# Four more k tiles of a down projection by seven products: a first group of half size in an encoder block's feed-forward part

## The chip, the core and the metric

The kernel runs on one core of a Trainium2 chip. The metric is the device time of one launch in microseconds (us), median of several runs. Engines are named as in the profile: PE is TensorE (the matrix unit), PEld its weight load, DVE is VectorE, ACT is ScalarE, POOL is GpSimd, SP is SyncE, which here only issues transfers.

## What is computed

One layer of an encoder over 256 tokens of width 2048, in float32. Attention with a window and a Fourier mixing part come first; the part that matters here is the feed-forward block behind them (5504 = 43 x 128 hidden features):

```python
h = _rmsnorm(x, norm2_g)
up = h @ w_up                                  # 2048 x 11008
gate, val = up[..., :D_FF], up[..., D_FF:]
gate = depthwise_conv(gate, dw_w, width 3) + dw_b
act = gelu(gate) * val                         # 256 x 5504
x = x + act @ w_down                           # 5504 x 2048: the down projection
y = _rmsnorm(x, normf_g)
```

## The kernel before

**Two parts of every operand.** A float32 matrix is split into a high part (rounded to a shorter format) and a low part (the rest). A product is three matmuls: high x high, low x high, high x low. The high part of a weight tile is made by ACT (a copy, L168, or L944 for the products' weights), the low part by DVE (a subtraction, L169 or L945). High and low tiles have three buffers each, shared by all kinds of units, so the split for item n + 2 can start when item n - 1 has left PE.

**Items.** From the feed-forward part on, the work is a list of items made by `ff_items`. One item is one stretch of matmuls on PE:

- *gate j* or *val j*: the up projection of one 128-feature tile, 32 matmuls (`still_weights`, L321), on 1 MB of weights.
- *product*: one of the seven products of a Strassen-like scheme for a group of the down projection. The activations of a group of 8 feature tiles are seen as a 2 x 2 block matrix (two halves of 4 tiles by two halves of 128 tokens), the weights likewise (two halves of 4 tiles by two column blocks of 512, `c` and `c + 2`). Seven products in place of eight, for each c in 0, 1. A product runs over 4 tiles, 3 matmuls each: 12 matmuls (`by_parts`, L1053 to L1055).
- *down*: a late unit. Feature tiles 32 to 39 go the plain way, in two sets of 4: per set, four units (one for each block of 512 columns), each 4 tiles x 2 token halves x 3 = 24 matmuls (`moving_weights`, L304 to L306).
- *last*: feature tiles 40 to 42, plain too, at the very end (`last_product`, L1192 to L1194), followed by the final norm.

Four groups cover tiles 0 to 31. While the 14 products of a group run, the up units of the next 8 tiles stand between them: `PATTERN` is `"uuu" + "su" * 13 + "s"` (u an up unit, s a product). After the last group's products come four late units, the six up units of tiles 40 to 42, four late units, four last units.

**What goes on beside PE.** `ff_step(n)` first issues what evicts the results of item n - 1 (`beside`), then the split of item n + 2, then what can wait (`behind`). The order is written out by hand; each engine works through its instructions in that order. Per up unit, DVE and ACT combine the two halves of the result (L833 to L836), run the convolution and GELU (L843 to L854) and multiply (L874; for the late and last tiles L866, with a split of the activations at L878 and L879). Per group, `operand` (L901, L902) and `operand_sums` make the seven left operands over seven steps. The products P1 and N5 stay in four banks of PSUM over all groups; the others are added to the residual `xs` or to the tiles Z when they end (`product_out`, L1022 to L1028). After the last product of a column block `shared_out` adds what is shared (L1036 to L1047, eight additions of 128x512 in three steps). `down_out` (L1060) adds a late unit to `xs`.

**The ring of product weights.** Per group and c, four weight tiles a, b, d, c are loaded by SP into two buffers (`ring_load`, L928), each when the split of an earlier one has freed its buffer. Sums of weights are made in part by POOL's accumulating transfers, which read a tile from HBM and add it in place: into b after `first_sums` (L959 and the transfer behind it), into the sum x after the split for N5 (L949) and after that for P6 (L951).

**Transfers of the other weights.** `split(i)` issues the load of unit i + 3 on SP (L152).

**The end.** `last_post` adds a last unit to `xs` (L1068), sums squares on ACT (L1072), and multiplies by the gain on POOL (L1080; the gain `gfb` is loaded by POOL at L1170, at the first late unit). The squares of the last column block are summed by DVE (L1085), those of blocks 1 and 2 are added by `other_squares` (DVE, L1090), and POOL takes the power (L1097); then the rows are scaled (L1106 to L1110) and stored.

**The q and k units** of the attention part also use `still_weights`. `QK_FIRST` says how many high and low parts each of them runs before it alternates.

Of the kernel before, what the change touches and what calls it, by code (L numbers as in the profile page):

```python
# [61 lines left out]

N_GROUPS = 4
LATE = [list(range(32, 36)), list(range(36, 40))]
LAST = list(range(40, NF))
# [3 lines left out]

PATTERN = "uuu" + "su" * 13 + "s"  # L70


def ff_items():


    def ups(tiles):
        return [(kind, j) for j in tiles for kind in ("gate", "val")]

    items = ups(range(8))
    for g in range(N_GROUPS):  # L80
# [4 lines left out]
        items += [todo[c].pop(0) for c in PATTERN]  # L85
        assert not any(todo.values())
    items += [("down", 0, c) for c in range(4)] + ups(LAST)
    items += [("down", 1, c) for c in range(4)] + [("last", c) for c in range(4)]
    return items


@with_exitstack
def block_kernel(
# [7 lines left out]
    w_out: bass.AP,  # L101
    w_up: bass.AP,
    w_down: bass.AP,
    w_down_late: bass.AP,
# [27 lines left out]
    for n, it in enumerate(items):  # L132
        if it[0] == "product":
            continue
        up_index[n] = len(units)
        if it[0] in ("gate", "val"):
            units.append((w_up[2 * it[1] + (it[0] == "val")], 2048))
            shifts.append((0, SHIFT))
            continue
        elif it[0] == "down":  # L140
            units.append((w_down_late[4 * it[1] + it[2]], 2048))
        else:
            units.append((w_down_last[it[1]], 512 * len(LAST)))
        shifts.append((0, 0))
# [589 lines left out]
    for n, (kind, h) in enumerate(QK_ORDER):  # L734

        def work(hi, lo):
            ps = st["ps", kind, h] = bank(mm, f"ps_{kind}{h}")
            still_weights(hi, lo, ps, range(NK), QK_FIRST.get(n, (0, 0)))

        unit(N_QK + n, work)  # L740
# [116 lines left out]
    def val_mult(j):  # L857
        va, ge = sums_of.pop(f"v{j}"), gate_out.pop(j)
        g, q = divmod(j, 8)
        if j >= 8 * N_GROUPS:  # L860
            if q % 2 == 0 or j == LAST[0]:
                tag = ("va", "va", "op_P1", "op_N3", "op_P7", "op_N5")[(j - 32) // 2]
# [7 lines left out]
        if q % 4 == 0:  # L870
            parts[g, q // 4] = fp.tile(
                [P, 4, S], F32, tag="va", name=f"va{g}k{q // 4}", bufs=3
            )
        nc.vector.tensor_tensor(parts[g, q // 4][:, q % 4, :], va, ge, ALU.mult)  # L874

# [17 lines left out]
    def block_of(g, name):  # L893
        k, t = PLACE[name]
        return parts[g, k][:, :, t * P : (t + 1) * P]

    def operand(g, name):

        o = fp.tile([P, 2, 4, P], F32R, tag=f"op_{name}", name=f"op_{name}", bufs=1)
        a = block_of(g, name)  # L900
        nc.scalar.activation(o[:, 0], a, AF.Copy)  # L901
        nc.vector.tensor_tensor(o[:, 1], a, f32(o[:, 0]), ALU.subtract)  # L902
        parts[name] = o
# [12 lines left out]

    ring, ring_tiles = [(g, c, w) for g in range(N_GROUPS) for c in range(2) for w in "abdc"], {}
    ring_next = [0]

    def weights_of(g, c, w):  # L920
        return w_down[(g * 2 + c) * 4 + "abcd".index(w)]

    def ring_load():
        if ring_next[0] < len(ring):
            key = ring[ring_next[0]]
            ring_next[0] += 1
            ring_tiles[key] = fp.tile([P, 2048], F32, tag="rawd", name="rawd%d%d%s" % key)
            nc.sync.dma_start(ring_tiles[key], weights_of(*key))  # L928
# [3 lines left out]
    def split_product(g, c, p):  # L932

        raw = {w: ring_tiles.get((g, c, w)) for w in "abcd"}
        x = ring_tiles["x"]
        src = {"P1": raw["a"], "N3": raw["d"], "P7": raw["b"], "P2": raw["c"]}.get(p, x)
        hi, lo = (
            wp.tile([P, 2176], F32R, tag=h, name=f"{h}_{p}_{g}{c}", bufs=3)[
                :, PRODUCT_SHIFT : PRODUCT_SHIFT + 2048
            ]  # L940
            for h in ("hi", "lo")
        )
        halves["product", g, c, p] = (hi, lo)
        nc.scalar.activation(hi, src, AF.Copy)  # L944
        nc.vector.tensor_tensor(lo, src, f32(hi), ALU.subtract)  # L945
        if p in ("P1", "P7", "N3", "P2"):
            ring_load()
        elif p == "N5":
            nc.gpsimd.dma_start(x, weights_of(g, c, "d"), accum_op=ALU.add)  # L949
        elif p == "P6":  # L950
            nc.gpsimd.dma_start(x, weights_of(g, c, "c"), accum_op=ALU.add)  # L951
        elif p == "N4" and (g, c) != (N_GROUPS - 1, 1):
            pending.append(lambda: first_sums(g + c, 1 - c))

    def first_sums(g, c):

        a, b = ring_tiles[g, c, "a"], ring_tiles[g, c, "b"]
        x = ring_tiles["x"] = fp.tile([P, 2048], F32, tag="sumw", name=f"sumw{g}{c}", bufs=1)
        nc.vector.tensor_tensor(x, a, b, ALU.add)  # L959
# [26 lines left out]
    def up_posts(n, kind, j, ps):  # L986
# [4 lines left out]
        else:  # L991
            at(beside, n + 1, scaled_sum, ps, f"v{j}")
            at(beside, n + 2, val_mult, j)
            if j % 8 == 7 and j < 8 * N_GROUPS:
                g = j // 8
                at(behind, n + 1, operand, g, "P1")
# [7 lines left out]
                at(behind, n + 7, operand, g, "P6")  # L1004
            if j >= 8 * N_GROUPS:
                at(behind, n + 2, act_parts, j)
# [41 lines left out]

    def by_parts(ps, o, hi, lo, first, last):

        for p in range(4):
            s = slice(p * 512, (p + 1) * 512)
            nc.tensor.matmul(ps, o[:, 0, p, :], hi[:, s], start=first and p == 0, stop=False)  # L1053
            nc.tensor.matmul(ps, o[:, 1, p, :], hi[:, s], start=False, stop=False)  # L1054
            nc.tensor.matmul(ps, o[:, 0, p, :], lo[:, s], start=False, stop=last and p == 3)  # L1055

# [8 lines left out]
    def last_post(c, b, ps, o=0, n=512):  # L1065
# [47 lines left out]

    pair = []
    for q in range(2):
# [17 lines left out]
    for n, it in enumerate(items):  # L1133
        if n < 2:
            continue
        if it[0] == "last":
            break
        if n in (8, 9):
            ring_load()
        if n == 13:  # L1140
            pending.append(lambda: first_sums(0, 0))
# [7 lines left out]
        if it[0] == "product":  # L1149
            kind, g, c, p = it  # L1150
            end = g == N_GROUPS - 1
            if (c, p) in held:
                by_parts(held[c, p], parts[p], *halves.pop(it), g == 0, end)
            else:
                ps = bank(mm, f"ps_{p}{g}{c}")
                by_parts(ps, parts[p], *halves.pop(it), True, True)
                at(beside, n + 1, product_out, g, c, p, ps)
            if end and p == "N4":
                for q in range(3):
                    at(behind, n + 1 + q, shared_out, c, q)  # L1160
        else:
            kind, g, c = it
# [58 lines left out]
def _layout(inp):  # L1221
# [40 lines left out]
    def rows_by(tiles, cols):  # L1262
# [4 lines left out]
    downs = [  # L1267
        rows_by(range(k, k + 4), c + n)
        for g in range(N_GROUPS)
        for c in (0, 512)  # L1270
        for k in (8 * g, 8 * g + 4)
        for n in (0, 1024)
    ]
    late = [rows_by(fs, 512 * c) for fs in LATE for c in range(4)]
    dw = f(inp["dw_w"]).reshape(3, NF, P).transpose(2, 1, 0).reshape(P, 3 * NF)
# [23 lines left out]
        "w_up": wup,  # L1299
        "w_down": np.stack(downs),  # L1300
        "w_down_late": np.stack(late),
# [22 lines left out]
```

## Time and profile before

| what | value |
|---|---|
| median of 3 runs (lowest, highest) | 947.45 us (947.23, 947.6) |
| the profiled execution | 947.17 us |
| its span, first to last instruction | 945.4 us |
| mean granted TensorE clock | 0.998 |
| PE, DVE, ACT, POOL busy | 935.7, 749.1, 534.2, 45.1 us |
| read from HBM | 208.79 MB, 223 GB/s over the span |

How to read it: a row of the list of groups names line, engine, operation, output and input, shape, count, then the busy time in us and the mean of one in ns, then the idle time of the engine ahead of it. A row of the chain gives start, length and what ran. A row of a timeline gives the same for one engine; what stands in brackets is the idle time ahead and what ended it. Rows of the list of waits give the total in us, how often, and the longest.

### The profile page before, as it was taken

How to read it: one execution, taken by the hardware profiler on the slowest of the kernel's cores; microseconds unless marked ns; L12 is line 12 of the kernel's file. 1: busy time of each engine (PE TensorE's matmuls, PEld its weight loads, DVE VectorE, ACT ScalarE, POOL GpSimd, SP SyncE). 2: the span in 40 equal slices, each digit the busy share in tenths (PEclk: the TensorE clock that was granted, in tenths of full speed). 3: DMA queues.
4: the chain of work that ended last, by engine and by line, in shares of the span. 5: the costliest groups of instructions: out<-in, count | busy, mean ns of one | idle time of the engine just before them, and what ended most of it. 6: DMA issues, size and time to landing. Idle time of an engine off the chain costs nothing.

```text
span 945.4 us, 12773 instructions
## 1 busy us (share of the span) xinstructions
PE 935.7 (99%) x5081; PEld 811.6 (86%) x5081; DVE 749.1 (79%) x932; ACT 534.2 (56%) x646; POOL 45.1 (5%) x59
## 2 busy tenths in 40 slices
PE   9999999999999999999999999999999999999996
PEld 7889998888888888888888888888888888888885
DVE  7668877566676689787898978988879979888776
ACT  7756766454454546556565555665556755553442
POOL 0100000000000000000000000000000000000002
PEclk9999999999999999999999999999999999999999
DMA  9964444446556675978778797877977697776532
GB/s 366 306 223 148 164 152 160 147 169 219 179 178 230 255 227 189 290 241 264 227 260 246 238 306 232 267 231 233 296 251 249 205 298 219 223 246 216 181 134 89
DMA packets 32189, 211.72 MB, mean 224 GB/s; under 512 B 3553, under 2 KB 4065, under 8 KB 8065
## 3 DMA queue, kind: packets, MB, share of 16 engines
q1 hardware_dynamic: 28448, 184.55, 53.2%
q0 software_dynamic: 3680, 26.35, 14.8%
q8 instruction: 40, 0.66, 0.3%
q14 instruction: 21, 0.16, 0.0%
HBM read 208.79 MB, written 2.10 MB: 223 GB/s over the span
## 4 chain that ended last, share of the span: by engine, by line
PE 98%; issue 1%; DMA 0%; DVE 0%; POOL 0%; ACT 0%; DVEq 0%; POOLq 0%; ACTq 0%
PE ps_gate L321 25%; PE ps_val L321 25%; PE ps_q L321 7%; PE ps_P L1055 3%; PE ps_P L1054 3%; PE ps_P L1053 3%; PE ps_a L306 2%; PE ps_a L304 2%; PE ps_k L321 2%; PE ps_N L1055 2%; PE ps_a L305 2%; PE ps_N L1054 2%; PE ps_N L1053 2%; PE ps_l L304 2%; PE ps_l L305 2%; PE ps_l L306 2%
## 5 line engine op out<-in xcount | busy, mean ns | idle before, releaser
L169 DVE TENSOR_TENSOR lo<-raw,hi 128x2048 fp32r<-128x2048 f32 (+1 forms) x133 | 302.7, 2276 | 53.8 <-ACT hi L168 53.7
L168 ACT ACTIVATE hi<-raw 128x2048 fp32r<-128x2048 f32 (+1 forms) x133 | 253.2, 1904 | 57.5 <-PE ps_l L305 22.8
L321 PE MATMUL ps_gate<-hU,hi 128*128 128x512 f32 x688 | 236.2, 389 | 0.0
L321 PE MATMUL ps_val<-hU,hi 128*128 128x512 f32 x688 | 236.2, 389 | 0.0
L321 PE MATMUL ps_gate<-hU,lo 128*128 128x256 f32 x688 | 189.9, 276 | 0.0
L321 PE MATMUL ps_val<-hU,lo 128*128 128x256 f32 x688 | 189.9, 276 | 0.0
L321 PEld LDWEIGHTS ps_gate<-hU,hi 128*128 128x128 f32 x688 | 129.2, 188 | 26.8
L321 PEld LDWEIGHTS ps_val<-hU,hi 128*128 128x128 f32 x688 | 129.1, 188 | 26.8
L321 PEld LDWEIGHTS ps_gate<-hU,lo 128*128 128x128 f32 x688 | 129.1, 188 | 1.1
L321 PEld LDWEIGHTS ps_val<-hU,lo 128*128 128x128 f32 x688 | 129.2, 188 | 1.1
L833 ACT ACTIVATE ft_g<-ps_gate 128x256 f32<-128x256 f32 x43 | 16.5, 384 | 120.0 <-PE ps_gate L321 119.8
L833 ACT ACTIVATE ft_v<-ps_val 128x256 f32<-128x256 f32 x43 | 16.5, 384 | 88.0 <-PE ps_val L321 88.0
L321 PE MATMUL ps_q<-hT,hi 128*128 128x512 f32 x192 | 66.2, 393 | 0.0
L321 PE MATMUL ps_q<-hT,lo 128*128 128x256 f32 x192 | 52.3, 277 | 0.0
L1053 PE MATMUL ps_P<-hi_P,op_P 128*128 128x512 f32 x128 | 49.8, 389 | 0.0
L1054 PE MATMUL ps_P<-hi_P,op_P 128*128 128x512 f32 x128 | 49.8, 389 | 0.0
L1055 PE MATMUL ps_P<-lo_P,op_P 128*128 128x512 f32 x128 | 49.8, 389 | 0.0
L945 DVE TENSOR_TENSOR lo_N<-sumw,hi_N 128x2048 fp32r<-128x2048 f32 x16 | 36.6, 2290 | 10.1 <-ACT hi_N L944 10.1
L321 PEld LDWEIGHTS ps_q<-hT,hi 128*128 128x128 f32 x192 | 35.7, 188 | 6.9
L304 PE MATMUL ps_a<-hi,cat 128*128 128x512 f32 x96 | 37.9, 395 | 0.0
L306 PE MATMUL ps_a<-lo,cat 128*128 128x512 f32 x96 | 37.5, 390 | 0.0
L835 DVE TENSOR_TENSOR fa_g<-ps_gate,ft_g 128x256 f32<-128x256 f32 x43 | 18.2, 422 | 24.3 <-ACT ft_g L833 24.3
(333 smaller groups left out, 1603.6 us busy)
## 6 DMA issues: line engine op xcount, KB each, us to landing
raw<-in_w_up SPq DMA_DIRECT2D x86, 1024.0 KB, 5.1
raw<-in_w_in SPq DMA_DIRECT2D x20, 1024.0 KB, 4.9
raw<-in_w_out SPq DMA_DIRECT2D x16, 1024.0 KB, 4.8
sumw<-in_w_down POOLq DMA_DIRECT2D x16, 1024.0 KB, 8.6
raw<-in_w_down_late SPq DMA_DIRECT2D x8, 1024.0 KB, 4.8
raw<-in_w_down_last SPq DMA_DIRECT2D x4, 768.0 KB, 4.2
ux<-in_w_u_x SPq DMA_DIRECT2D x3, 768.0 KB, 9.2
xs<-in_x SPq DMA_DIRECT2D x4, 512.0 KB, 16.5
```

The source lines that it names most:

```text
L168: nc.scalar.activation(hi[:, 0:n], raw[:, 0:n], AF.Copy)
L169: nc.vector.tensor_tensor(lo[:, 0:n], raw[:, 0:n], f32(hi[:, 0:n]), ALU.subtract)
L304: nc.tensor.matmul(ps, ah, wh, start=first and q == q0, stop=False)
L305: nc.tensor.matmul(ps, al, wh, start=False, stop=False)
L306: nc.tensor.matmul(ps, ah, wl, start=False, stop=last and q == q0 + len(kk) - 1)
L321: nc.tensor.matmul(ps[:, x], (hi, lo)[i][:, k * P : (k + 1) * P], hk(k)[:, x], start=n == 0 and k == 0, stop=n == len(order) - 1 and k == ...
L833: nc.scalar.activation(tmp, ps[:, S : 2 * S], AF.Copy)
L835: nc.vector.tensor_tensor(add, ps[:, 0:S], tmp, ALU.add)
L945: nc.vector.tensor_tensor(lo, src, f32(hi), ALU.subtract)
L1053: nc.tensor.matmul(ps, o[:, 0, p, :], hi[:, s], start=first and p == 0, stop=False)
L1054: nc.tensor.matmul(ps, o[:, 1, p, :], hi[:, s], start=False, stop=False)
L1055: nc.tensor.matmul(ps, o[:, 0, p, :], lo[:, s], start=False, stop=last and p == 3)
```

## The change

The down projection gets five groups in place of four: a first one of half size (two halves of 2 tiles, tiles 0 to 3) and four of full size (tiles 4 to 35). Only tiles 36 to 39 remain for late units, four of them, and these no longer follow the products: in the last group's pattern they stand among the last products, as do the six up units of tiles 40 to 42. A product of the half group is 6 matmuls on half a weight tile (128x1024). In the last group, the products P2 and N4 of column block c are not evicted: the late unit for c (0 or 1) adds to their two banks, and one `down_out` evicts both. The closing sums of c = 1 are issued after P6 already, one step in every two items. The first loads of the ring come at items 2 and 3, the first sum at item 5. `gfb` is loaded at the late unit for c = 1. At the end, the squares of blocks 1 and 2 of the second token half are added by POOL, each as it comes, in place of one DVE operation. All q and k units but two now run one high part ahead.

```diff
-QK_FIRST = {0: (1, 0), 2: (1, 0), 4: (1, 0), 5: (1, 0), 6: (1, 0), 8: (2, 2), 10: (2, 2), 12: (2, 2), 14: (1, 0)}
+QK_FIRST = {n: (2, 2) if n in (8, 12) else (1, 0) for n in range(16)}
...
-N_GROUPS = 4
-LATE = [list(range(32, 36)), list(range(36, 40))]
+GROUPS = [(0, 2), (4, 4), (12, 4), (20, 4), (28, 4)]
+LATE = list(range(36, 40))
...
-PATTERN = "uuu" + "su" * 13 + "s"
+PATTERNS = ["uuu" + "su" * 13 + "s"] * (len(GROUPS) - 1)
+PATTERNS += ["uuu" + "su" * 6 + "sd" + "su" * 5 + "sdsdd"]
...
+    firsts = [first for first, _ in GROUPS] + [LATE[0], NF]
+    items = ups(0, firsts[1])
+    for g, pattern in enumerate(PATTERNS):
         todo = {
-            "u": ups(range(8 * g + 8, 8 * g + 16)),
+            "u": ups(firsts[g + 1], firsts[g + 2]),
             "s": [("product", g, c, p) for c in range(2) for p in PRODUCTS[c]],
+            "d": [("down", c) for c in (0, 2, 1, 3)],
         }
...
-    items += [("down", 0, c) for c in range(4)] + ups(LAST)
-    items += [("down", 1, c) for c in range(4)] + [("last", c) for c in range(4)]
+    return items + [("last", c) for c in range(4)]
...
     def operand(g, name):
         o = fp.tile([P, 2, 4, P], F32R, tag=f"op_{name}", name=f"op_{name}", bufs=1)
+        o = o[:, :, 0 : GROUPS[g][1], :]
...
+    def ring_tile(g, tag, name, bufs):
+        t = fp.tile([P, 2048], F32, tag=tag, name=name, bufs=bufs)
+        return t[:, 0 : 512 * GROUPS[g][1]]
...
-    def by_parts(ps, o, hi, lo, first, last):
-        for p in range(4):
+    def by_parts(ps, o, hi, lo, n, first, last):
+        for p in range(n):
...
+        if (c, b) == (1, 1):
+            nc.gpsimd.tensor_tensor(
+                ssq3[:, b, 3:4], ssq3[:, b, 3:4], ssq3[:, b, 1:2], ALU.add
+            )
...
-        if n in (8, 9):
+        if n in (2, 3):
             ring_load()
-        if n == 13:
+        if n == 5:
             pending.append(lambda: first_sums(0, 0))
...
+            elif end and p in ("P2", "N4"):
+                ps = joined[c, p] = bank(mm, f"ps_{p}{g}{c}")
+                by_parts(ps, parts[p], *halves.pop(it), GROUPS[g][1], True, False)
...
-            if end and p == "N4":
+            if end and p == ("N4", "P6")[c]:
                 for q in range(3):
-                    at(behind, n + 1 + q, shared_out, c, q)
+                    at(behind, n + 1 + (1 + c) * q, shared_out, c, q)
...
-            ps = [bank(mm, f"ps_l{g}{c}{b}") for b in range(2)]
+            if c < 2:
+                ps = [joined.pop((c, p)) for p in ("P2", "N4")]
+            else:
+                ps = [bank(mm, f"ps_l{c}{b}") for b in range(2)]
             for b in range(2):
-                moving_weights(hi, lo, 512, LATE[g], act.get, b, ps[b], True, True)
+                moving_weights(hi, lo, 512, LATE, act.get, b, ps[b], c >= 2, True)
             at(beside, n + 1, down_out, c, ps)
-            if (g, c) == (0, 0):
+            if c == 1:
                 gfb = fp.tile([P, D], F32, tag="sumw", name="gfb", bufs=1)
                 nc.gpsimd.dma_start(gfb, normf_g.partition_broadcast(P))
...
-    v = other_squares(1, add_squares(1, 0, 256, ssq3[:, 1, 3:4], 4))
+    v = add_squares(1, 0, 256, ssq3[:, 1, 3:4], 4)
+    nc.gpsimd.tensor_tensor(v, v, ssq3[:, 1, 2:3], ALU.add)
```

The rest of the diff lays the weights out to match (a `w_down_two` of eight half tiles, `w_down` of 32 tiles, `w_down_late` of four) and passes the group's size along.

More of the change, by code (lines that the diff above doesn't have):

```diff
@@ L68, with group_of, ups @@
 ]
-PATTERN = "uuu" + "su" * 13 + "s"
-def ff_items():
[L76 to L80, printed above, removed]
+PATTERNS = ["uuu" + "su" * 13 + "s"] * (len(GROUPS) - 1)
+PATTERNS += ["uuu" + "su" * 6 + "sd" + "su" * 5 + "sdsdd"]
+def group_of(j):
+    for g, (first, n) in enumerate(GROUPS):
+        if j < first + 2 * n:
+            return (g, *divmod(j - first, n))
+    return None
+def ff_items():
+    def ups(first, end):
+        return [(kind, j) for j in range(first, end) for kind in ("gate", "val")]
+    firsts = [first for first, _ in GROUPS] + [LATE[0], NF]
+    items = ups(0, firsts[1])
+    for g, pattern in enumerate(PATTERNS):
         todo = {
-            "u": ups(range(8 * g + 8, 8 * g + 16)),
+            "u": ups(firsts[g + 1], firsts[g + 2]),
             "s": [("product", g, c, p) for c in range(2) for p in PRODUCTS[c]],
+            "d": [("down", c) for c in (0, 2, 1, 3)],
         }
-        items += [todo[c].pop(0) for c in PATTERN]
-        assert not any(todo.values())
-    items += [("down", 0, c) for c in range(4)] + ups(LAST)
-    items += [("down", 1, c) for c in range(4)] + [("last", c) for c in range(4)]
-    return items
+        items += [todo[c].pop(0) for c in pattern]
+        assert not (todo["u"] or todo["s"]), (g, todo)
+    return items + [("last", c) for c in range(4)]
 @with_exitstack
@@ L140, in block_kernel @@
         elif it[0] == "down":
-            units.append((w_down_late[4 * it[1] + it[2]], 2048))
+            units.append((w_down_late[it[1]], 2048))
         else:
@@ L737, in work @@
             ps = st["ps", kind, h] = bank(mm, f"ps_{kind}{h}")
-            still_weights(hi, lo, ps, range(NK), QK_FIRST.get(n, (0, 0)))
+            still_weights(hi, lo, ps, range(NK), QK_FIRST[n])
         unit(N_QK + n, work)
@@ L869, in val_mult @@
             return
[L870 to L874, printed above, removed]
+        g, half, q = group_of(j)
+        if q == 0:
+            parts[g, half] = fp.tile([P, 4, S], F32, tag="va", name=f"va{g}k{half}", bufs=3)
+        nc.vector.tensor_tensor(parts[g, half][:, q, :], va, ge, ALU.mult)
     def act_parts(j):
@@ L913, in operand_sums @@
             tt(a01, a00, a01, ALU.add)
-    ring, ring_tiles = [(g, c, w) for g in range(N_GROUPS) for c in range(2) for w in "abdc"], {}
+    ring, ring_tiles = [(g, c, w) for g in range(len(GROUPS)) for c in range(2) for w in "abdc"], {}
     ring_next = [0]
     def weights_of(g, c, w):
-        return w_down[(g * 2 + c) * 4 + "abcd".index(w)]
+        n = c * 4 + "abcd".index(w)
+        return w_down_two[n] if g == 0 else w_down[8 * (g - 1) + n]
+    def ring_tile(g, tag, name, bufs):
+        t = fp.tile([P, 2048], F32, tag=tag, name=name, bufs=bufs)
+        return t[:, 0 : 512 * GROUPS[g][1]]
     def ring_load():
@@ L951, in split_product @@
             nc.gpsimd.dma_start(x, weights_of(g, c, "c"), accum_op=ALU.add)
-        elif p == "N4" and (g, c) != (N_GROUPS - 1, 1):
+        elif p == "N4" and (g, c) != (len(GROUPS) - 1, 1):
             pending.append(lambda: first_sums(g + c, 1 - c))
@@ L957, in first_sums @@
         a, b = ring_tiles[g, c, "a"], ring_tiles[g, c, "b"]
-        x = ring_tiles["x"] = fp.tile([P, 2048], F32, tag="sumw", name=f"sumw{g}{c}", bufs=1)
+        x = ring_tiles["x"] = ring_tile(g, "sumw", f"sumw{g}{c}", 1)
         nc.vector.tensor_tensor(x, a, b, ALU.add)
@@ L993, in up_posts @@
             at(beside, n + 2, val_mult, j)
-            if j % 8 == 7 and j < 8 * N_GROUPS:
-                g = j // 8
+            if j + 1 in [first + 2 * n for first, n in GROUPS]:
+                g = group_of(j)[0]
                 at(behind, n + 1, operand, g, "P1")
@@ L1054, in by_parts @@
             nc.tensor.matmul(ps, o[:, 1, p, :], hi[:, s], start=False, stop=False)
-            nc.tensor.matmul(ps, o[:, 0, p, :], lo[:, s], start=False, stop=last and p == 3)
+            nc.tensor.matmul(ps, o[:, 0, p, :], lo[:, s], start=False, stop=last and p == n - 1)
     def down_out(c, pss):
@@ L1111, in scaled @@
         nc.sync.dma_start(out[b * P : (b + 1) * P, k : k + n], y)
-    pair = []
+    pair, joined = [], {}
     for q in range(2):
@@ L1267, in _layout @@
     downs = [
-        rows_by(range(k, k + 4), c + n)
-        for g in range(N_GROUPS)
+        rows_by(range(k, k + m), c + n)
+        for first, m in GROUPS
         for c in (0, 512)
-        for k in (8 * g, 8 * g + 4)
+        for k in (first, first + m)
         for n in (0, 1024)
     ]
-    late = [rows_by(fs, 512 * c) for fs in LATE for c in range(4)]
+    late = [rows_by(LATE, 512 * c) for c in range(4)]
     dw = f(inp["dw_w"]).reshape(3, NF, P).transpose(2, 1, 0).reshape(P, 3 * NF)
```

28 lines of the change are left out of this document (15 added, 13 removed).

## The prediction, made before the changed kernel ran

> **What bounds the kernel now.** I read the page first: busy shares, then the chain that ended last. Then the list of what TensorE (PE) waited for, because a busy share of 99% can hide short stalls.
>
> ```profile
> PE 935.7 (99%) x5081; PEld 811.6 (86%) x5081; DVE 749.1 (79%) x932; ACT 534.2 (56%) x646; POOL 45.1 (5%) x59
> PE 98%; issue 1%; DMA 0%; DVE 0%; POOL 0%; ACT 0%; DVEq 0%; POOLq 0%; ACTq 0%
> ```
>
> ```profile
> PE ps_warm L249 <- POOL ones L241: 1.0, 1, 1.0
> PE ps_u L383 <- ACT hT L256: 0.6, 1, 0.6
> ```
>
> The second fence is the whole list of PE's waits: 1.6 us, both at the very start. From the first weights on PE never waits for an engine or a transfer. So the time is the number of matmuls times their pitch, plus a short start and a tail after the last matmul. A change gains only by taking matmuls away or shortening the tail, and it loses only if something that is now hidden comes late.
>
> **The pitch.** Successive matmuls overlap in the trace, so the printed duration of one is not its cost. The cost is the distance between starts, which the chain in order of time gives.
>
> ```profile
> 828.36 5.44 PE ps_gate L321 x32
> 836.52 5.44 PE ps_val L321 x32
> 866.47 5.46 PE ps_gate L321 x32
> ```
>
> A gate or value unit (32 matmuls) takes 5.44 us, and the next begins 8.16 us after it. The 2.72 us between are one product: 4 k tiles of 3 matmuls, 12 in all, so 0.2267 us for each 512-wide matmul. The four late units follow the last product, from 836.52 + 5.44 + 2.72 = 844.68 to 866.47: 21.79 us for 96 matmuls, 0.227 each. The two ways of doing the down projection pay the same per matmul, and opening one more product has no price of its own (at most 0.01 us).
>
> **The change: matmuls.** Four k tiles cost 4 units x 24 = 96 matmuls by the plain way. As a half group they cost 14 products x 2 tiles x 3 = 84. Twelve matmuls go: 12 x 0.2267 = **-2.72 us**. Nothing else on PE changes in number.
>
> **Order of the q and k units.** In sixteen units only the order of the same matmuls changes. PE waits for nothing there, so there is no wait to remove.
>
> ```profile
> 59.49 5.47 PE ps_q L321 x32
> 65.41 5.49 PE ps_q L321 x32
> ```
>
> The first of these has the plain alternation, the second one high part ahead: 0.02 us apart. Eight units change, so between -0.2 and +0.2 us; I take 0.
>
> **What hides the vector work.** Every weight needs a high part on ACT and a low part on DVE before PE may use it. The half group adds 14 half-size splits and drops four full ones.
>
> ```profile
> L169 DVE TENSOR_TENSOR lo<-raw,hi 128x2048 fp32r<-128x2048 f32 x130 | 297.5, 2288 | 52.3 <-ACT hi L168 52.1
> L377 DVE TENSOR_TENSOR lo<-ux,hi 128x1024 fp32r<-128x1024 f32 x4 | 4.9, 1222 | 0.7 <-ACT hi L376 0.7
> L835 DVE TENSOR_TENSOR fa_v<-ps_val,ft_v 128x256 f32<-128x256 f32 x43 | 18.2, 423 | 14.3 <-ACT ft_v L833 14.3
> L1028 DVE TENSOR_TENSOR xs<-ps_N,xs 128x512 f32<-128x512 f32 x16 | 10.9, 684 | 0.0
> ```
>
> ```profile
> 360.00:469.00 109.00, 109.00 (x588) 94.29 (x587) 90.38 (x90) 66.11 (x65) 4.26 (x5) 1.00 0.77 244
> 735.00:845.00 110.00, 110.00 (x593) 95.13 (x592) 97.81 (x109) 66.27 (x66) 4.85 (x6) 1.00 0.76 235
> ```
>
> In the windows view the columns are sum, PE, weight loads, DVE, ACT, POOL, clock, DMA share, GB/s. The first window is the first group, the second the last group. In the **half group** PE's time for the same steps falls to 14 x 1.36 + 13 x 5.44 = 89.8 us. DVE's 90.38 loses 14 x (2.29 - 1.22) = 15.0 on splits, 1.1 on the sum of two weights, and 11 x (0.68 - 0.42) = 2.9 on operands: 71.4 us, 80% of PE's time against 83% now. In the **last group** two up units go out of the stretch (4.0 us of DVE each: a split of 2.29, four 0.42-us operations), four late units come in (2.29 + 2 x 0.68 each, 14.6), four products lose their eviction because they share a bank with a late unit (-2.7), and the closing sums of the second column now fall inside (8 x 0.68 = 5.5): 97.8 - 8.0 + 14.6 - 2.7 + 5.5 = 107.2 us. PE's time there is 14 x 2.72 + 15 x 5.44 = 119.7, so 90% against 89% now. DVE does not become the bound in either stretch.
>
> An average can still hide one late split. How early are they? In a quiet pair:
>
> ```profile
> 379.56 5.44 PE ps_val L321 x32
> 382.23 2.29 DVE L169 TENSOR_TENSOR lo<-raw,hi 128x2048 fp32r<-128x2048 f32 x1
> 387.72 5.44 PE ps_gate L321 x32
> ```
>
> The low part for the unit at 387.72 was ready at 384.52, 5.0 us after the unit before it began. In the half group the next unit begins after 6.80 us instead of 8.16, so some 1.8 us are left. The tightest place that I found is in the last group:
>
> ```profile
> 743.53 2.28 DVE L169 TENSOR_TENSOR lo<-raw,hi 128x2048 fp32r<-128x2048 f32 x1
> 745.73 0.69 DVE L902 TENSOR_TENSOR op_N<-va3k,op_N 128x512 fp32r<-128x512 f32 x1
> 746.83 0.28 PE L321 MATMUL ps_gate<-hU,lo 128*128 128x256 f32 x1
> ```
>
> There 1.0 us is left (ready 745.81, used 746.83). The changed kernel has the same steps at this place, since the first three up units and the first six pairs of the last group keep their order. In the half group's own operand steps the DVE work shrinks with the window. So I cost the vector work at nothing; if the cover fails by a microsecond or two at one place, that is the price, once. No bank is waited for either: the late unit for column block 3 takes the two banks of block 2, freed a whole product and a unit earlier.
>
> **Transfers that move.** The first weights of the half group are loaded six items earlier, on SP's queue ahead of loads for up units; the final gain is loaded later, on POOL's queue, behind the last accumulating transfers.
>
> ```profile
> raw<-in_w_up SPq DMA_DIRECT2D x86, 1024.0 KB, 5.1
> gfb<-in_normf_g POOLq DMA_DIRECT2D x1, 1024.0 KB, 4.6
> ```
>
> Up weights are loaded three units ahead (3 x 5.44 = 16.3 us) and land in 5.1, so two half loads in front, each at most another 5.1, use up only part of the 11 us that are left. The gain can be issued when the last product's weight is split. From there PE still has that product, two late units and the first last product, 2.72 + 2 x 5.44 + 2.04 (9 matmuls) = 15.6 us, before POOL multiplies by it: 4.6 us of landing fit. Both cost nothing.
>
> **The tail.** On POOL two 128x1 additions are new, and one DVE operation (L1090) goes.
>
> ```profile
> 935.81 0.19 ACT L1072 ACTIVATION_READ_ACCUMULATOR junkc<-xs 128x1 f32 x1
> 937.04 0.19 ACT L1072 ACTIVATION_READ_ACCUMULATOR junkc<-xs 128x1 f32 x1
> ```
>
> ```profile
> 936.76 0.48 DVE L1085 CUSTOM_DVE_ANT_0 z_P<-xs,ssq 128x256 f32<-128x256 f32 x1
> 937.17 0.08 DVE L1085 DVE_READ_ACCUMULATOR2_ANT ssq<- 128x1 f32 x1
> 937.37 0.27 DVE L1090 TENSOR_SCALAR ssq<-ssq 128x1 f32<-128x1 f32 x1
> 937.56 0.41 DVE L1068 TENSOR_TENSOR xs<-ps_e,xs 128x256 f32<-128x256 f32 x1
> 938.00 0.48 DVE L1085 CUSTOM_DVE_ANT_0 z_P<-xs,ssq 128x256 f32<-128x256 f32 x1
> ```
>
> ```profile
> 931.06 0.57 POOL L1097 TENSOR_TENSOR rstd<-ssq,half_pow 128x1 f32<-128x1 f32 x1 [1.11 <-DVE ssq L1090]
> 938.58 0.55 POOL L1097 TENSOR_TENSOR rstd<-ssq,half_pow 128x1 f32<-128x1 f32 x1 [4.55 <-DVE ssq L1085]
> ```
>
> ```profile
> 937.06 0.28 PE L1194 MATMUL ps_e<-lo,act 128*128 128x256 f32 x1
> ```
>
> A 128x1 operation on POOL took 0.55 us here; the additions are not in this trace, so I price them like it. The first can start at 936.0 (ACT's result) and ends about 936.6, ahead of its use at 936.76. The second can start at about 937.3 and ends about 937.9, when DVE wants it at 938.0; meanwhile DVE, free of L1090, does its addition up to 0.15 us earlier. Queued behind each on POOL is only the other and the power. Both ends: -0.15 us, or +0.55 if one addition lies wholly on the path. I take 0.
>
> The sum: 947.17 (the profiled execution: span 945.4 and 1.8 around it) - 2.72 = 944.45. The median of the runs is 947.45, 0.28 above the profiled one, which gives 944.73. I forecast **944.6 us**.
>
> **A rule that speaks against it.** The tail's rows show when POOL and DVE get in each other's way:
>
> ```profile
> 931.15 0.69 DVE L1068 TENSOR_TENSOR xs<-ps_e,xs 128x512 f32<-128x512 f32 x1 [0.17 <-PE ps_e L1194]
> 932.74 1.29 POOL L1080 TENSOR_TENSOR xs<-xs,gfb 128x512 f32<-128x512 f32 x1 [1.11 <-ACT junkc L1072]
> 932.77 1.81 DVE L1106 SCALAR_TENSOR_TENSOR xs<-xs,rstd,gfb 128x512 f32<-128x512 f32 x1
> 939.43 2.07 DVE L1106 SCALAR_TENSOR_TENSOR xs<-xs,rstd,gfb 128x512 f32<-128x512 f32 x3
> ```
>
> Three such DVE operations alone took 2.07 us, one beside POOL's took 1.81: about 1.1 us lost. As a mechanism of this kernel: if a new POOL addition starts just ahead of a DVE operation on SBUF, DVE stands for its 0.55 us; both on the path give 944.6 + 1.1 = 945.7, one gives 945.15. Against it: during the second addition DVE adds from PSUM, and such an addition at 931.15, beside POOL's power at 931.06, took its ordinary 0.69. The Trainium skill, page "SBUF — State Buffer", section "Who interferes with whom", says that POOL and a DVE operation with two SBUF inputs take one shared port as an exclusive lock, and the later one waits to the end. By that rule the new additions could hold the squares at 936.76; the trace agrees in the 1.81 us.
>
> **The rivals.**
> (a) *Late splits.* The last group, at 90%, with 1.0 us of slack, or the half group, with 1.8, makes PE wait a few times. For: the closing sums now run among splits. Against: all the sums above. Price 0.5 to 2.5 us: 945.1 to 947.1.
> (b) *The POOL lock*, as priced: 945.15 to 945.7.
> (c) *The half group does not halve.* If a product had a fixed cost of 0.19 us, 14 more of them would eat the 2.72: 947.2. Against: the 0.01 us above.
> (d) *Slower: accumulating transfers land late in the half group.*
>
> ```profile
> sumw<-in_w_down POOLq DMA_DIRECT2D x16, 1024.0 KB, 8.6
> rawd10b<-in_w_down POOLq DMA_DIRECT2D x1, 1024.0 KB, 10.5
> ```
>
> POOL adds a weight tile from HBM into the sum between N5's split and P6's, and again between P6's and N4's. In three of four cases these now lie 2 x 6.80 = 13.6 us apart, not 16.3. N5's split takes some 2.7 of them, and a late split still has some 4 us before PE wants it, so PE waits once a landing takes over about 14.9 us. Each microsecond above costs up to 3. From 16.4 us of landing on, the result is over 0.2% slower (3 x 1.55 = 4.6 us); at 17 it is 951. Against: 8.6 is the median and 10.5 the worst for twice the bytes.
>
> **How the numbers follow.** About 0.2% (1.9 us) is what a measurement can tell from no change. My forecast, 944.2 to 945.1, has 0.72: PE's arithmetic is exact and only hidden work can spoil it. (b) 0.05, (a) 0.13, (c) 0.04, (d) 0.06. Faster by over 0.2%, below 945.55: 0.72, 0.05 and 0.05 of (a), 0.82. Same: the rest of (a) and (c), 0.12. Slower: 0.06. The range goes from 944.0 (both gains of order and tail) to 946.4 (most of (a)), which leaves out 0.06, 0.04 and some 0.05 of (a).
>
> **What would show it.** Right: PE's list of waits still has only the two rows of the start; products of the first group last 1.36 us in the chain, so their pairs recur every 6.80; the last matmul ends 2.7 us earlier; the tail after it is as long as now (945.4 - 937.34 = 8.1 us). Wrong: a PE wait for a low part (L181 or L962 of the changed kernel) proves (a); a DVE split of the first group that waits for a transfer, with PE waiting behind it, proves (d); a longer stretch between the last matmul and the last power on POOL proves (b).

## The result, and the profile after

The changed kernel takes **945.76 us** (median of 18 runs, 945.2 to 947.13) against 947.4 for the kernel before (18 runs, 946.81 to 948.04): a ratio of 0.9982, 95% interval 0.9975 to 0.9988. It is faster by 1.6 us. The forecast was 944.6 with a range of 944.0 to 946.4, so the sign is as forecast, the time lies in the range, and 1.2 us of the expected gain are missing.

The page of the kernel after: its busy time by engine, and the chain that ended last by engine.

```profile
PE 934.7 (99%) x5069; PEld 809.9 (86%) x5069; DVE 759.8 (81%) x948; ACT 541.4 (57%) x659; POOL 50.6 (5%) x67
...
PE 98%; DVE 1%; DMA 0%; issue 0%; ACT 0%; DVEq 0%; POOLq 0%; POOL 0%; ACTq 0%
```

Its PE has twelve matmuls fewer, 5069 for 5081, as the change says. At 0.2267 us each they should take 2.72 us with them, but PE's busy time fell by 1.0 only. The list of what PE waited for does not tell where the rest is:

```profile
PE ps_warm L261 <- POOL ones L253: 1.0, 1, 1.0
PE ps_u L395 <- ACT hT L268: 0.2, 1, 0.2
```

It is whole, and again has only the two rows of the start. So PE waits for nothing and yet is longer busy than its matmuls account for: the matmuls themselves must have become longer. The chain in order of time shows where. First the half group (start, length, what ran):

```profile
317.12 0.23 PE ps_P L1070
...
318.48 5.44 PE ps_val L333 x32
...
325.28 5.44 PE ps_gate L333 x32
...
332.08 5.44 PE ps_val L333 x32
```

A pair recurs every 6.80 us, so a product of the half group takes 1.36, exactly half. Then the last group:

```profile
842.08 5.44 PE ps_gate L333 x32
...
850.24 0.23 PE ps_P L316
850.47 0.24 PE ps_P L317
...
855.71 0.23 PE ps_P L1070
...
858.47 5.60 PE ps_val L333 x32
...
866.85 5.60 PE ps_gate L333 x32
...
875.22 5.60 PE ps_val L333 x32
...
883.59 5.60 PE ps_gate L333 x32
...
891.97 5.60 PE ps_val L333 x32
```

L316 and L317 are the first late unit, L1070 the product behind it. From there on a unit of the same 32 matmuls takes 5.60 us, not 5.44, and a pair recurs every 8.37, not 8.16. I call this the **slow stretch**. It runs from 855.8 to 902.3, into the second token half of the late unit for block 2; the product and the first half of the late unit behind that are slow again (905.9 to 910.5); then all is normal. Lengths there above the usual ones: five up units at 0.16, the products between them at 0.055, the edges; together 1.3 us. I call a start **slow** when it comes later behind the one before than the usual 226.7 ns for 512 columns or 113.3 ns for 256, and count what it is late by. Behind 266 us of the span, and without one break of 0.1 us near 267 that both kernels have, slow starts add up to 0.18 us in before and to 1.44 in after.

What else differs between the normal stretch ahead of it and the slow one of equal length? The windows view (sum, PE, weight loads, DVE, ACT, POOL, clock, DMA share, GB/s), the normal stretch first:

```profile
801.20:847.60 46.40, 46.40 (x255) 40.34 (x254) 41.26 (x43) 27.56 (x30) 1.72 (x2) 1.00 0.75 234
855.80:902.20 46.40, 46.40 (x241) 39.48 (x240) 40.69 (x45) 26.61 (x23) 1.72 (x2) 1.00 0.69 222
```

Then two groups by form (busy time, mean ns of one, idle time), in the normal stretch and, in the fence behind it, in the slow one:

```profile
L333 PE MATMUL ps_val<-hU,hi 128*128 128x512 f32 x48 | 16.5, 389 | 0.0
...
L333 PEld LDWEIGHTS ps_val<-hU,lo 128*128 128x128 f32 x48 | 9.0, 188 | 0.1
```

```profile
L333 PE MATMUL ps_val<-hU,hi 128*128 128x512 f32 x48 | 16.9, 395 | 0.0
...
L333 PEld LDWEIGHTS ps_val<-hU,lo 128*128 128x128 f32 x48 | 9.0, 188 | 0.1
```

The granted clock is 1.00 in both, the transfers and DVE do less in the slow one, the weight loads are equal at 188 ns. Only the matmuls are longer, 395 ns for 389, with nothing in these views that would explain it.

The span fell by 1.7 us, from 945.4 to 943.7: -2.72 for the matmuls, +1.26 for slow starts, +0.17 because the v units began that much later (27.10 for 26.93; in the runs below it lies between 26.82 and 27.56 whatever the change), -0.05 on the q and k units, -0.31 behind the start of the last matmul. That is -1.65.

### The profile page after: what moved, and what is told of

Same layout as the page of the kernel before. It is cut to its first block, busy times and chain, and to the rows that moved or that the text cites. A ratio compares the mean times of both kernels' runs of the same rounds, so it can differ in the third digit from the quotient of the medians.

```text
span 943.7 us, 12802 instructions
## 1 busy us (share of the span) xinstructions
PE 934.7 (99%) x5069; PEld 809.9 (86%) x5069; DVE 759.8 (81%) x948; ACT 541.4 (57%) x659; POOL 50.6 (5%) x67
## 4 chain that ended last, share of the span: by engine, by line
PE 98%; DVE 1%; DMA 0%; issue 0%; ACT 0%; DVEq 0%; POOLq 0%; POOL 0%; ACTq 0%
PE ps_val L333 25%; PE ps_gate L333 25%; PE ps_q L333 7%; PE ps_P L1071 3%; PE ps_P L1072 3%; PE ps_P L1070 3%; PE ps_N L1071 3%; PE ps_N L1072 3%; PE ps_N L1070 3%; PE ps_a L318 2%; PE ps_a L316 2%; PE ps_k L333 2%; PE ps_a L317 2%; PE ps_s L637 1%; PE ps_o L709 1%; PE ps_ff L316 1%
## 5 line engine op out<-in xcount | busy, mean ns | idle before, releaser
L181 DVE TENSOR_TENSOR lo<-raw,hi 128x2048 fp32r<-128x2048 f32 (+1 forms) x129 | 293.4, 2275 | 40.5 <-ACT hi L180 40.3
L180 ACT ACTIVATE hi<-raw 128x2048 fp32r<-128x2048 f32 (+1 forms) x129 | 245.5, 1903 | 41.5 <-PE ps_a L317 13.5
L1071 PE MATMUL ps_P<-hi_P,op_P 128*128 128x512 f32 x144 | 56.2, 390 | 0.0
L1070 PE MATMUL ps_P<-hi_P,op_P 128*128 128x512 f32 x144 | 56.1, 389 | 0.0
L1072 PE MATMUL ps_P<-lo_P,op_P 128*128 128x512 f32 x144 | 56.0, 389 | 0.0
L962 DVE TENSOR_TENSOR lo_N<-sumw,hi_N 128x2048 fp32r<-128x2048 f32 (+1 forms) x20 | 41.5, 2076 | 9.4 <-ACT hi_N L961 9.2
L1071 PE MATMUL ps_N<-hi_N,op_N 128*128 128x512 f32 x108 | 42.1, 390 | 0.0
L1070 PE MATMUL ps_N<-hi_N,op_N 128*128 128x512 f32 x108 | 42.0, 389 | 0.0
L1072 PE MATMUL ps_N<-lo_N,op_N 128*128 128x512 f32 x108 | 42.0, 389 | 0.0
```

The costliest lines, as they stand in the source:

```text
L180: nc.scalar.activation(hi[:, 0:n], raw[:, 0:n], AF.Copy)
L181: nc.vector.tensor_tensor(lo[:, 0:n], raw[:, 0:n], f32(hi[:, 0:n]), ALU.subtract)
```

## The experiments

The late units' high and low tiles begin at offset 0 of their buffers (in elements of 4 bytes), the products' at 28 (`PRODUCT_SHIFT`), the up units' at 0 and 16 (`SHIFT`). In late units and products these tiles are what the matmuls stream (`moving_weights`, `by_parts`); in up units they are what PE loads as weights (`still_weights`). In before no late unit stands directly ahead of a product; in after two do. The candidates: the offset of the late units (A), their place directly ahead of a product (B), the banks that they now share with products (C), the denser work of DVE, ACT and the transfers beside the last group (D).

**1. Late units at the products' offset.**

```diff
         elif it[0] == "down":
             units.append((w_down_late[it[1]], 2048))
+            shifts.append((PRODUCT_SHIFT, PRODUCT_SHIFT))
+            continue
```

> The changed kernel, with the high and low parts of the late units at the products' place in their buffers (offset 28 in place of 0). In the changed kernel every matmul between the product behind the first late unit and the last late units starts 4.5 ns later than elsewhere, 1.28 us in all. If the offset decides (theory A), these matmuls go back to 226.7 and 113 ns and the span falls by about 1.2 us against the changed kernel, to 942.5. If only the order of units decides (theory B), if the shared banks decide (rival C), or if the denser work of DVE, ACT and the transfers decides (rival D), the slow stretch stays and the time stays within 0.2 us of the changed kernel.

Measured: 944.61 us, ratio 0.9971 (0.9961 to 0.9981), span 943.7. The chain of this kernel:

```profile
858.87 5.44 PE ps_val L335 x32
...
867.02 5.44 PE ps_gate L335 x32
```

The slow stretch is gone, every late unit and product at its usual length, slow starts 0.20 us in all, with the same work beside PE as in after: D falls. But the span did not shrink with it: this execution began 0.46 later (27.56), and a new row stands in the list of PE's waits, with DVE's rows for it:

```profile
PE ps_e L1223 <- DVE lo L183: 0.4, 1, 0.4
```

```profile
919.01 1.76 DVE L1212 TENSOR_TENSOR lo<-raw,hi 128x1536 fp32r<-128x1536 f32 x1 [2.65 <-ACT hi L1211]
920.68 1.28 DVE L1079 TENSOR_TENSOR xs<-ps_l,xs 128x512 f32<-128x512 f32 x2
921.88 1.75 DVE L183 TENSOR_TENSOR lo<-raw,hi 128x1536 fp32r<-128x1536 f32 x1
```

The last of these rows is the low part for the third of the four last units, ready at 923.63. PE, now ahead of its old time, began the last products at 918.54 and wants it 20 matmuls later, at 923.07. The first row, the split of the fourth, stands ahead of it in DVE's order and waited 2.65 us: ACT's high part came only when the fourth's weights had landed, at 917.49.

**2. An up unit behind the first late unit.** The last pattern is `"uuu" + "su" * 6 + "sdu" + "su" * 3 + "ssu" + "sdsdd"` in place of `"uuu" + "su" * 6 + "sd" + "su" * 5 + "sdsdd"`: the first late unit (d) has an up unit behind it, not a product; the second still has a product.

> The changed kernel, with an up unit and not a product behind the first late unit (two products stand together later instead). Theory B (a late unit directly ahead of a product starts the slow stretch): no slow matmuls from there to the next late unit, about 1.1 us gained, span near 942.6. Theory A (offset): the same as B or the slow stretch stays, since the up unit has yet another offset. Rivals C (shared banks) and D (denser work): the slow stretch stays. If two products together cost a wait, PE's list of waits shows it.

Measured: 944.95 us, ratio 0.9974 (0.9964 to 0.9983), span 942.8. The stretch is gone but for 0.10 us behind the late unit that still has a product behind it; another 0.2 us went at the last units, where the third's low part came late as in run 1. The up unit behind the first late unit takes 5.46 us, the next one 5.44 again:

```profile
855.61 5.46 PE ps_val L333 x32
...
863.79 5.44 PE ps_gate L333 x32
```

So either edit is enough: A and B are two halves of one condition.

**3. Own banks for the late units.** The products P2 and N4 are evicted as in the earlier groups, and all late units open banks of their own.

> The changed kernel without the shared banks: P2 and N4 of the last group are evicted, and the late units for blocks 0 and 1 have banks of their own. Rival C (adding a late unit to a product's bank starts the slow stretch): the slow matmuls are gone, span near 942.5. Theories A and B and rival D: the slow stretch stays, 1.2 us; DVE has four more evictions of 0.68 us, which stay hidden, so the time is within 0.3 us of the changed kernel.

Measured: 946.02 us, ratio 0.9984 (0.9974 to 0.9993), span 944.3. The stretch stands where it was, 1.20 us, with units of 5.60. C falls. (The third last unit's low part came late here too, and PE lost 0.5 us by it.)

**4. The kernel before, with one late unit moved** ahead of the last group's product N5 of the second column block; nothing else of the change.

```diff
+    items.remove(("down", 0, 1))
+    items.insert(items.index(("product", 3, 1, "N5")), ("down", 0, 1))
```

> The kernel before, with one late unit of the first set (column block 1) moved ahead of the last group's product N5 of the second column block; nothing else. Theories A and B: the product behind it and all units up to the end of the products get slow by 4.5 ns a matmul: 6 products of 12 and 5 up units of 32 matmuls, 232 x 4.5 ns = 1.0 us, so the span rises to about 946.4. Rivals C and D: no slow stretch, within 0.2 us of the kernel before.

Measured: 948.43 us, ratio 1.0012 (1.0002 to 1.0021), span 946.9. One moved unit makes a kernel slower that does the same matmuls:

```profile
809.71 5.60 PE ps_val L323 x32
...
818.09 5.60 PE ps_gate L323 x32
...
843.21 5.60 PE ps_val L323 x32
```

The stretch goes from 807.0 to 853.5, again 1.20 us and again into a late unit. With the first two runs this shows the cause from both sides.

**5. The third last unit split before the fourth**, on top of run 1, to take the new wait away.

```diff
-    split_last(3)
+    split_last(2)
...
-        split_item(n + 2)
+        split_item(n + 3 if items[n] == ("last", 0) else n + 2)
```

> After, with the late units at offset 28 (as in the run of that name, which read 944.61 us), and with the third of the last units split into a ring tile ahead of the fourth, instead of the fourth ahead of the third. Theory A: the wait of 0.81 + 0.34 us (less two usual starts of 0.227, so 0.70) that TensorE had there for the low part of the third last unit goes, because DVE makes that low part at 919.0 to 920.8 of the span instead of 921.9 to 923.6, and the fourth's low part, now the later one, is needed 2.04 us later. The last twelve products take 16.6 us instead of 17.4, the span is 943.0, the time 943.9 (943.6 to 944.2). Rival: the last units' loads arrive in an order that makes the third as late as the fourth was, then the wait stays, at 944.6; or DVE's next reader, the additions of the last products, is what ends the kernel, then the wait goes and the tail grows by the same.

Measured: 944.35 us, ratio 0.9969 (0.9957 to 0.998), span 942.6. DVE's rows:

```profile
914.30 1.76 DVE L183 TENSOR_TENSOR lo<-raw,hi 128x1536 fp32r<-128x1536 f32 x1 [0.49 <-ACT hi L182]
915.98 1.75 DVE L1212 TENSOR_TENSOR lo<-raw,hi 128x1536 fp32r<-128x1536 f32 x1
...
919.74 1.76 DVE L183 TENSOR_TENSOR lo<-raw,hi 128x1536 fp32r<-128x1536 f32 x1 [0.60 <-ACT hi L182]
```

The third's low part (L1212) is ready at 917.73, five us ahead of use, and DVE no longer stands idle for the fourth's load. PE's wait is gone. The time is 0.15 above the interval that was expected.

**6, 7, 10. Which offsets?** Late units at 0 and 16 (run 6), products at 0 like the late units (7), late units at 16 and 16 (10).

```diff
         elif it[0] == "down":
             units.append((w_down_late[it[1]], 2048))
+            shifts.append((0, SHIFT))
+            continue
```

> After, with the late units' high part at offset 0 as now and the low part at 16, like the up units (both at 0 in after; the products stay at 28 and 28). Theory A1 (a product behind a unit whose buffers stand at another offset than its own starts the slow stretch): the stretch from 855.8 to 902 of the span stays, 1.2 us in all, time 945.8. Theory A2 (it is the late units' high and low part at the same offset 0 that starts it): the stretch is gone, time 944.6, with the wait for the third last unit's low part as in the run with late units at offset 28.

```diff
-PRODUCT_SHIFT = 28
+PRODUCT_SHIFT = 0
```

> After, with the products' buffers at offset 0 instead of 28, so that products and late units stand alike at 0 and 0. A1 (a difference between product and late unit is needed): no slow stretch behind the late units, 944.6. A2 (offset 0 for both parts is itself the trouble): every product, 70 of them, can start the stretch, then it begins at the first product at about 300 of the span and holds for as long as it did in after per product; bounded by all matmuls from there on at 4.5 ns each, 2,700 x 4.5 ns = 12 us, up to 957 us.

> After, with both parts of the late units at offset 16 (0 in after; the products stay at 28). So far: alike at 28 and 28 no slow stretch, alike at 0 and 0 none behind late units but 24 ns at each switch between product and up unit, late at 0 before product at 28 a stretch of 1.20 us, late parts at 0 and 16 one of 1.77 us. Theory (any other offset than that of the product behind it starts the stretch): it is there from 855.8 to 902 of the span, time 945.8. Rival (what counts is offset 0 in the late unit's first part): it is gone, time 944.6 to 944.9.

Run 10's edit is run 6's with `(SHIFT, SHIFT)`. Measured: run 6 945.92 us (ratio 0.9983, 0.9974 to 0.9992); run 7 947.49 (1.0002, 0.9992 to 1.0011); run 10 944.93 (0.9977, 0.9967 to 0.9986). An up unit of the last group in run 6, then in run 10, and one of the second group in run 7:

```profile
858.31 5.60 PE ps_val L335 x32
```

```profile
858.29 5.44 PE ps_val L335 x32
```

```profile
426.43 5.46 PE ps_val L333 x32
```

Run 6 is the worst of the late units: slow starts from the first matmul of the first late unit, at 849.8, through the last late unit and into the last products, at 920.9, 1.77 us. Run 10 has no stretch; each late unit is itself some 0.05 us longer (slow starts 0.41 in all), and products and up units are normal. In run 7 the late units do no harm, but every switch between a product and an up unit costs: four or five matmuls of 228 to 236 ns behind each of them, 0.025 for a product and 0.022 for a unit, 3.20 us over the kernel. So neither of the two theories written for these runs holds. It is not that any other offset than the product's starts it (run 10), and it is not that only equal parts at 0 do (run 6). What holds is a table: products at 28 cost nothing beside up units or beside late units at 28; late units at 16 and 16 beside them cost 0.05 us each; late units at 0 and 0 set off slow matmuls at the next product, and at 0 and 16 with their own first matmul, and these last for tens of us.

**8. The orders of the q and k units alone**, in the kernel before.

> Before, with only the new orders of the q and k units. The ninth q or k unit, which took 5.60 us in before and 5.45 in after, takes 5.45: span 945.25 against 945.4, too little for the time of one run to show; the rest of the span is as before. Rival: the 0.15 us came from elsewhere in after, and the unit takes 5.60 again.

Measured: 947.24 us in the one run, span 945.4. The same unit in before, here, and in after:

```profile
112.72 5.60 PE ps_q L321 x32
```

```profile
112.84 5.45 PE ps_q L321 x32
```

```profile
112.93 5.45 PE ps_q L333 x32
```

The orders do take 0.15 us off this unit, but others give most of it back: from the first matmul of the v units to the first gate unit it is 228.68 us before, 228.63 here and 228.63 in after. Net 0.05.

**9. The tail as before, in the kernel after**: `other_squares` back on DVE, no additions on POOL.

> After, with the sums of squares of the tail added as in before (one DVE instruction over two columns, no POOL additions). By the trace of after the two POOL additions took 0.19 us each, not the 0.55 that the prediction's bound took, and lie 0.8 us ahead of the power's input: nothing to gain or lose, end of the power 2.07 us behind the start of the last matmul as in before (2.01 in after), time 945.8 within 0.15. Rival: the additions on POOL held the chain up, then the end of the power comes 0.2 to 0.5 us sooner and the time is 945.3 to 945.6.

Measured: 945.73 us, ratio 0.9983 (0.9973 to 0.9992), span 943.7: no difference in time. The tail of after, for comparison with before's:

```profile
934.84 0.19 POOL L1097 TENSOR_TENSOR ssq<-ssq 128x1 f32<-128x1 f32 x1 [2.04 <-ACT junkc L1089]
936.12 0.19 POOL L1240 TENSOR_TENSOR ssq<-ssq 128x1 f32<-128x1 f32 x1 [1.09 <-ACT junkc L1089]
937.13 0.55 POOL L1118 TENSOR_TENSOR rstd<-ssq,half_pow 128x1 f32<-128x1 f32 x1 [0.82 <-DVE ssq L1106]
```

```profile
935.67 0.28 PE L1221 MATMUL ps_e<-lo,act 128*128 128x256 f32 x1
```

The additions take 0.19 us each and the second ends 0.8 ahead of the power's start. From the start of the last matmul to the end of the power it is 2.01 us (2.07 before, 2.21 in run 9); to the end of the span 8.03 (8.34 before). Over all profiles it is 8.03 to 8.13 with POOL's additions (ten profiles) and 8.23 to 8.35 with the old tail (before and runs 4, 8, 9). That is a gain of 0.1 to 0.3 us, too small for the times to confirm: against before most of it lies behind the power, against run 9 all of it ahead of the power's end.

**11 and 12. After, and the version of run 5, side by side on one chip.**

> The kernel after, unchanged, beside the next run on the same chip: 945.8 us (945.6 to 946.0), with the slow stretch of 1.20 us at 855.8 to 902.

> The kernel with late units at offset 28 and the third last unit split early, unchanged, on the same chip as the kernel after. If the slow stretch is what the prediction missed: 1.1 to 1.4 us less than after, 944.4 to 944.7, with a span near 942.6. If the first run's 944.35 was the spread of few runs: within 0.3 of after, 945.5 to 946.0.

Measured: after 945.28 us (ratio 0.9978, 0.9969 to 0.9986; span 943.9), run 5's version **944.09** (0.9966, 0.9952 to 0.9979; span 942.3). 1.2 us less, as expected from the stretch; this version is faster than both kernels. In this execution of after, too, the low part for the third last unit came late:

```profile
922.07 1.75 DVE L181 TENSOR_TENSOR lo<-raw,hi 128x1536 fp32r<-128x1536 f32 x1
```

It was ready at 923.82 and PE lost 0.3 us there, two usual starts having become 0.45 and 0.34. In the execution read first the margin was 0.42 us, in before 1.27.

## Why the prediction was right in sign and short in size

**Right: twelve matmuls fewer, and the half group halves.** Products of 1.36 us, pairs every 6.80. Rival (c) did not happen. Without the slow starts the forecast is met: where 944.6 was forecast, run 1 reads 944.61, and run 5's version, which has all of the change in it and an earlier split besides, 944.35 and 944.09. That after itself lies in the range is luck: the room above 945.1 was left for late splits and for POOL holding DVE up, and what filled it was slow starts, which no rival named.

**Wrong: the pitch.** The step that failed is "Nothing else on PE changes in number", with "The two ways of doing the down projection pay the same per matmul, and opening one more product has no price of its own" in front of it. The number was right and the two ways do pay the same while each stands among its own kind. But I took the pitch from stretches with a settled order and carried it to an order that the trace of before did not hold: a late unit directly ahead of a product. That neighbour costs 1.26 us of slow starts. Runs 1 and 2 remove it from either side, run 4 makes it in before, run 3 clears the shared banks. The last matmul began 1.4 us earlier, not 2.7. The trace of before did hold the hint, in one q unit of 5.60 us among others of 5.44 to 5.58 (in that one, every 512-wide matmul takes 233 ns to the next start and every 256-wide one 117, as in the up units of the slow stretch), and the 0.02 us at 866.47 that I quoted without asking what it was.

The Trainium skill, page "TensorE: Matmul & The Clock Gate", section "Wait — 56ns, not 53.3ns?", gives the distance of starts in a warm array as a function of the columns alone, 215.7 ns at 512. The trace disagrees: 226.7 ns here for nearly all 512-wide matmuls, and 231 in the slow stretch at the same granted clock of 1.00.

**Right: DVE is hidden in both groups.** The windows of the half group and of the last group of after:

```profile
316.82:406.58 89.76, 89.76 (x502) 78.33 (x501) 73.03 (x88) 51.73 (x64) 4.26 (x5) 1.00 0.76 236
798.39:919.36 120.97, 120.97 (x619) 103.03 (x617) 106.74 (x115) 68.88 (x65) 4.85 (x6) 1.00 0.72 226
```

DVE is busy 73.0 us for 71.4 expected in the half group, and 106.7 for 107.2 in the last. No split was late in either.

**Rival (a), late splits**, did come, but behind both groups and not at the place that I had called the tightest. The closing order of the last units (the fourth's split ahead of the third's, waiting for the fourth's load) had 1.27 us to spare in before; as the last products move up by 1.4 us and the low part by only 0.5, 0.42 is left, and it is used up in some executions. What that costs goes with when the fourth's load lands: 0.7 us in run 1, 0.5 in run 3, 0.3 in run 11, 0.2 in run 2, nothing in the execution of after read first. I searched the groups that change for slack, not the part that only moves.

**The tail**: the price of an addition on POOL was wrong, 0.55 us taken from the power where it is 0.19; the value taken, 0, was near, the bounds (-0.15 to +0.55) leaned to the wrong side: it came out at -0.31, of which 0.06 lie ahead of the power's end. Rival (b) did not show.

**Transfers**: half tiles that accumulate landed in 5.3 us in the median, full ones in 8.3, so rival (d) did not happen. The first two half loads on SP landed in 7.1 and 7.9 us, not in the 5.1 that I had called the most (5.1 was a median); no unit came late by it. The orders of q and k: -0.05 in -0.2 to +0.2.

## What to carry to other kernels

Where one engine bounds the time and never waits, a list of waits cannot show a loss: compare the length of the same unit of work across the whole timeline, and take any that differ as a price to be explained before work is reordered. When units of another kind are put between others, look at the unit lengths behind each new neighbour and try its buffer offsets. Equal ones cost nothing between late units and products here, but putting the products at 0 for it cost 3.20 us at their switches with up units, so each neighbour has to be looked at; no rule for the offsets came out. And after a gain ahead of the end, look again at what the end waits for: loads and splits there need not move with it.

## What the hardware showed that I had not expected

A 512-wide matmul started 226.7 ns after the one before it nearly everywhere, and 231 on average for 46 us on end, at a full granted clock, with equal weight loads and with less going on beside it. Behind late units the state is set off by where the operands of a few matmuls lie in their buffers and by what follows them, and it outlasts them: units of another kind with unchanged operands stay slow until the second half of a late unit (in run 6 the last products) ends it. It is not tied to late units: the q unit of 5.60 us in before has the same starts, with no late unit near, and run 8 took it away by changing nothing but the order of matmuls in the q and k units. The Trainium skill, page "SBUF — State Buffer", section "Operand start alignment", lets an operand start at any multiple of its element size and says that this is about legality, not speed; every offset here is legal, and they differ by up to 3.2 us of slow starts in the kernel. What in the chip keeps this state was not found: the runs show which neighbours and offsets set it off, not why.
